# One substitution for both head groups in the delta-net stage of a two-block kernel, and its late weight splits on VectorE

## The chip, the cores and the metric

The kernel runs on one core of one Trainium2 chip. The metric is the device time of one execution in microseconds (us). The engines are named as in the profile: PE is TensorE, DVE is VectorE, ACT is ScalarE, POOL is GpSimd, SP is SyncE, which issues the transfers from memory. PEld is PE's weight load.

## The reference

Two transformer blocks run over 512 tokens of width 1024. The second one adds 16 learned tokens in front, runs a SwiGLU, a mixer and another SwiGLU. The mixer adds a latent attention and a gated delta net, each with a sigmoid gate. The change lies in the delta net, which works on chunks of 64 tokens with 8 heads of 64:

```python
lmat = jnp.where(tri_strict, jnp.einsum('bhncd,bhnsd->bhncs', kb, kc) * decay, 0.0)
eye = jnp.eye(CHUNK, dtype=jnp.float32)
tmat = lax.linalg.triangular_solve(eye + lmat, jnp.broadcast_to(eye, lmat.shape),
                                   left_side=True, lower=True)
u_c = tmat @ (vc * bc[..., None])
w_c = tmat @ (kb * jnp.exp(gc)[..., None])
intra = jnp.einsum('bhncd,bhnsd->bhncs', qc, kc) * decay

def step(state, inp):
    q_i, k_i, u_i, w_i, g_i, a_i = inp
    v_new = u_i - w_i @ state
    o_i = (q_i * jnp.exp(g_i)[..., None]) @ state + a_i @ v_new
    ...
```

Beside it, in the same stretch of the kernel, the gates (`gate_mla`, `gate_gdn`, `z`) are dense products of the normalized hidden state with parts of `w_in`.

## The kernel before, in words

**Precision of the dense products.** A weight tile `raw` of 128x1024 is split in two parts: ACT writes `wh` (rounded), and another engine writes `wl = raw - wh`. Every dense product is three matmuls (`wh` with the high and the low part of the input, `wl` with the high part). `Ctx.stock` (line 434) makes the splits ahead of use: two `raw` tiles may be in flight, and `wh` and `wl` have three buffers each, so a new `wh` waits until PE has finished the weight three places before. The list `mix_items` (line 1493) gives the order of the weights, and its last field says which engine makes `wl`: `None` is DVE, `po` is POOL.

**The delta-net stage.** `gdn` (line 2039) runs 10 units: five token tiles `t` (the first has 16 tokens, the others 128, two chunks each) for each of two head groups `G` of four heads. Unit `u` is `2 t + G`. Each unit passes six generators:

- `prep_a`: POOL makes `gr`; PE transposes k, q (`ptm`) and v (`ptv`); PE sums the decays (`pd`) and ACT makes `E = exp`; DVE and POOL make `vk`, `kb`, `qn`, `qe`, `kd`.
- `prep_b`: PE transposes `kb`, `qn` (`ptb`), ACT copies them to `kqT`, PE multiplies (`pkq`), DVE makes `LT` (the strictly lower matrix, transposed) and `AT`.
- `base`: inverts the 16x16 diagonal blocks of `LT` by substitution. POOL cuts the blocks out (`lm`), DVE folds them into `L16`. Then come 15 steps of three dependent DVE instructions (`STREAM_SHUFFLE XR<-X`, `XR<-XR,L`, `X<-X,XR`), which work on four heads and 1 to 15 columns, so on 4 to 60 elements in each of 128 partitions. POOL spreads the result into `TT`.
- `inverse`: two levels that join blocks: PE transposes `TT` (`ptt`), ACT copies to `Tm`, PE multiplies with `CT` (made by POOL), ACT copies to `Pm`, PE multiplies (`pr`), DVE subtracts from `TT`.
- `factors`: PE makes `pu` (the u and w of the reference), ACT copies to `uw`.
- `scan`: the recurrence over chunks with the state `S` (`pws`, `vn`, `pS`, `po`), then norm and gate of the output.

**The fill.** `filler` (line 1702) is a seventh generator beside them. It issues the dense products `mm<-x,wh` of the z and gate columns (24 matmuls of 512 columns for each weight tile), and then of `w_o2`. DVE multiplies each finished product (`z` or `gate <- mm,bcu`) and ACT applies tanh.

**What sets the order.** Every instruction is emitted by a planner (`Ctx.run`, line 377, and `Clock.pump`, line 185) that holds a clock with costs for each engine. A generator's step runs when the planner finds its inputs ready; the generators are ranked `scan, factors, inverse, base, prep_b, prep_a, fill`. Each engine then runs its own list strictly in that order, and waits on semaphores for the others. The costs know nothing of two engines that slow each other down. Pools give buffers by tag: a tile of a tag waits until the oldest one of that tag has been read for the last time.

Of the kernel before, what the change touches and what calls it, by code (L numbers as in the profile page):

```python
# [10 lines left out]
F32 = mybir.dt.float32  # L11
# [3 lines left out]
ALU = mybir.AluOpType  # L15
AX = mybir.AxisListType  # L16
PSUM = bass.MemoryType.PSUM

P = 128
D = 1024  # L20
KT = D // P
S = 512
NM = 16
T = S + NM
# [1452 lines left out]


HM = 8
DEEP = 3  # L1480

GATES = 3


def b3(ap, n, axis=2):

    sh = list(ap.shape)
    v = ap.unsqueeze(axis)
    sh.insert(axis, n)
    return v.to_broadcast(sh)  # L1490


def mix_items(c):
    po = c.nc.gpsimd
    it = [("w_mix", m, 0, 1024, None) for m in (2, 0, 1, 3)]
    it += [("w_mix", m, 0, 1024, po) for m in [*range(4, 16), *range(20, 20 + GATES), *range(16, 20), *range(20 + GATES, 36)]]
    it += [("w_o2", m, o, 512, None) for o in (0, 512) for m in range(KT)]
    it += [("w_mo", m, 0, 1024, None) for m in range(KT)]
    return it
# [539 lines left out]
def gdn(c, keep, pool, psp, st):  # L2039
# [25 lines left out]
    U = {}  # L2065
# [4 lines left out]
    def prep_a():  # L2070
        yield ("setup",)
        for u, (t, G) in enumerate(units):
            if u >= DEEP:
                yield ("factors", u - DEEP)
            if u > 3:
                yield ("scan", u - 4)
            to, n = TT_B[t]
            ts_, hs = slice(to, to + n), hb(G)
            na = 2 if t else 1

            gr = pool.tile([P, 4, P], F32, tag="gr", name=c.nm("gr"))
            nc.gpsimd.tensor_tensor(
                out=gr[:n, :, :n].rearrange("p (a b) m -> p a b m", a=2),
                in0=b3(b3(M_incl[:n, :n], 2, 1), 2, 1), in1=b3(par_of(g[:n, t, hs]), n, 3), op=ALU.mult)

            kq = pool.tile([P, 2, 4, 64], F32, tag="kq", name=c.nm("kq"))
            yield from room("ga")
            pt = PS("ga", "ptm")
            for i, nm in enumerate("kq"[:na]):
                for f in range(2):  # L2090
                    c.tr(pt[:n, (2 * i + f) * P : (2 * i + f + 1) * P], st[nm][2 * G + f][:, ts_], c.ident)
            nc.scalar.copy(kq[:n, :na].rearrange("p a h d -> p (a h d)"), pt[:n, : 256 * na])
            yield from room("ga")
            pv = PS("ga", "ptv")
            for f in range(2):
                c.tr(pv[:n, f * P : f * P + P], st["v"][2 * G + f][:, ts_], c.ident)
            vk = pool.tile([P, 4, 2, 64], F32, tag="vk", name=c.nm("vk"), bufs=DEEP)
            kd = tok("kd", 4)
            nc.vector.tensor_mul(vk[:n, :, 0], pv[:n, :256].rearrange("p (h d) -> p h d", h=4), b3(beta[:n, t, hs], 64, 2))
            if u:  # L2100
                yield ("E", u - 1)
            yield from room("ga", gr)
            E = pool.tile([P, 4, P], F32, tag="E", name=c.nm("E"))
            pd = v4(PS("ga", "pd"))[:n, :, :n]
            c.mm(pd, M_after[:n, :n], gr[:n, :, :n], True, False)
            c.mm(pd, identb[:n, :n], b3(nmb[:n, :n], 4, 1), False, True)
            nc.scalar.activation(E[:n, :, :n], pd, AF.Exp)
            kb = tok("kb")
            nc.vector.tensor_mul(kb[:n], kq[:n, 0], b3(sc[0][:n, t, hs], 64, 2))
            d = U[u] = dict(vk=vk, kd=kd, E=E, kb=kb)  # L2110
            if t:
                qn, qe = d["qn"], d["qe"] = tok("qn"), tok("qe", DEEP)
                nc.vector.tensor_mul(qn[:n], kq[:n, 1], b3(sc[3][:n, t, hs], 64, 2))
                nc.gpsimd.tensor_tensor(out=vk[:n, :, 1], in0=kq[:n, 0], in1=b3(sc[1][:n, t, hs], 64, 2), op=ALU.mult)
                nc.gpsimd.tensor_tensor(out=qe[:n], in0=kq[:n, 1], in1=b3(sc[4][:n, t, hs], 64, 2), op=ALU.mult)
            nc.gpsimd.tensor_tensor(out=kd[:n], in0=kq[:n, 0], in1=b3(sc[2][:n, t, hs], 64, 2), op=ALU.mult)
            c.mark(("tok", u), kb, *([qn] if t else []))

    def prep_b():
        for u, (t, G) in enumerate(units):  # L2120
# [4 lines left out]
            E = d["E"]  # L2125
            na = 2 if t else 1

            kqT = pool.tile([P, 2, 2, P], F32, tag="kqT", name=c.nm("kqT"))
            yield from room("gb")
            pt = PS("gb", "ptb").rearrange("p (f a m) -> p f a m", f=2, a=2)  # L2130
            for f in range(2):
# [20 lines left out]

    def base():

        for u, (t, G) in enumerate(units):
            yield ("LT", u)
            n, d = TT_B[t][1], U[u]
            r = 32 if t == 0 else P
            X, R_, L16 = (pool.tile([P, 4, 16], F32, tag=x_, name=c.nm(x_)) for x_ in ("X", "XR", "L16"))
            if t:  # L2160
                lm = v4(c.cp.tile([P, T], F32, tag="h7", name=c.nm("lm"))[:, :S])
                nc.gpsimd.tensor_tensor(out=lm, in0=d["LT"], in1=b3(blk[:, 24:], 4, 1), op=ALU.mult)
                nc.vector.tensor_reduce(out=L16, in_=lm.rearrange("p h (b i) -> p h i b", i=16), op=ALU.add, axis=AX.X)
            else:
                nc.gpsimd.memset(L16[:r], 0.0)
                nc.vector.tensor_mul(L16[:n], d["LT"][:n, :, :n], b3(blk[:n, 24 : 24 + n], 4, 1))
            nc.gpsimd.tensor_copy(X[:r], b3(blk[:r, 8:24], 4, 1))
            for i in range(15, 0, -1):
                o = slice(i, 16)
                nc.vector.stream_shuffle(R_[:r, :, o], X[:r, :, o], [16 * (q // 16) + i for q in range(32)])  # L2170
                nc.vector.tensor_mul(R_[:r, :, o], R_[:r, :, o], L16[:r, :, i : i + 1].to_broadcast([r, 4, 16 - i]))
                nc.vector.tensor_sub(X[:r, :, o], X[:r, :, o], R_[:r, :, o])
            TT = pool.tile([P, 4, P], F32, tag="TT", name=c.nm("TT"), bufs=3)
            if t:
                nc.gpsimd.tensor_tensor(out=TT.rearrange("p h (b i) -> p h b i", i=16), in0=b3(X, 8, 2),
                                        in1=b3(b3(blk[:, :8], 16, 2), 4, 1), op=ALU.mult)
            else:
                nc.gpsimd.tensor_copy(TT[:n, :, :n], X[:n])
            d["TT"] = TT
            c.mark(("base", u), TT)  # L2180
            if t == 0:
                c.mark(("inv", u), TT)
            st["based"] = u == len(units) - 1
            yield

    second = lambda a, b: a.rearrange("p q (k two b) -> p q k two b", two=2, b=b)[:, :, :, 1, :]

    def inverse():

        for u, (t, G) in enumerate(units):  # L2190
# [3 lines left out]
            for i in range(2 if t else 0):  # L2194
                CT = pool.tile([P, 4, P], F32, tag="CT", name=c.nm("CT"), bufs=2)
                nc.gpsimd.tensor_tensor(out=CT, in0=LT, in1=b3(lev[:, i, :], 4, 1), op=ALU.mult)
                Tm = pool.tile([P, 4, P], F32, tag="Tm", name=c.nm("Tm"), bufs=2)
                yield from room("gi", TT)
                pt_ = v4(PS("gi", "ptt"))
                for q in range(4):  # L2200
# [3 lines left out]
                pp = v4(PS("gi", "pp"))  # L2204
                for q in range(4):
                    c.mm(pp[:, q], CT[:, q], Tm[:, q], True, True)
                Pm = pool.tile([P, 4, P], F32, tag="Pm", name=c.nm("Pm"), bufs=2)
                nc.scalar.copy(Pm, pp)
                b = 16 << i
                yield from room("gi", Pm)  # L2210
# [379 lines left out]
```

## Time and profile before

| | us |
|---|---|
| median of 3 runs | 2119.61 (2118.64 to 2121.54) |
| the profiled execution | 2118.18 |
| its span, first to last instruction | 2116.4 |
| delta-net stage within the span | 1366 to 1672 |

The page gives each engine's busy time as a share of the span. The stretch that the change touches lies between 1366 us, where the attention of the mixer has ended, and 1672 us, where the products of `w_o2` for the latent attention are done. In a timeline a row begins with start and duration in us; in brackets stands how long the engine sat idle before it, and who released it. In a group by shape the mean duration is in ns. [...]

### The profile page before, as it was taken

The numbers are of one execution on the slowest core, as the hardware profiler recorded it, in microseconds if no ns is written. First come the engines' busy times: TensorE is split into PE (matmuls) and PEld (weight loads), VectorE is DVE, ScalarE is ACT, GpSimd is POOL, SyncE is SP. The second block draws the span as 40 slices with busy tenths as digits, with TensorE's granted clock in tenths as the row PEclk, the third lists the DMA queues.
The fourth block names the chain that finished last, engine by engine and source line by source line (L and its number), as shares of the span: only waits on it lengthen the run. The fifth ranks groups of instructions, "written<-read, shape, count | busy, mean of one in ns | idle before, by whom it ended". The sixth has DMA issues, their size and how long they took to land. (4 is left out here: it accounts for less than half of the span.)

```text
span 2116.4 us, 30687 instructions
## 1 busy us (share of the span) xinstructions
PE 2028.2 (96%) x12029; PEld 1755.6 (83%) x12029; DVE 1198.3 (57%) x2503; ACT 848.1 (40%) x1615; POOL 482.7 (23%) x399
## 2 busy tenths in 40 slices
PE   8999999979999989999999999988889999999998
PEld 6888888867888889999999988856667788888887
DVE  5665564388667573333333677588897653434333
ACT  4444443266565552222222576522233342323222
POOL 3111110154343050000010444344553220000000
PEclk9999999989999999999999999999999999999999
DMA  4222222321211212222224210122001742222332
GB/s 153 80 81 80 80 78 73 100 80 61 70 61 57 90 63 90 91 90 90 85 91 151 74 51 31 56 65 75 16 31 41 248 145 96 93 100 90 93 102 75
DMA packets 61728, 178.67 MB, mean 84 GB/s; under 512 B 8400, under 2 KB 11600, under 8 KB 61584
## 3 DMA queue, kind: packets, MB, share of 16 engines
q1 hardware_dynamic: 60208, 175.54, 25.6%
q8 instruction: 94, 1.54, 0.3%
q10 hardware_dynamic: 1376, 1.18, 0.2%
q14 instruction: 50, 0.41, 0.1%
HBM read 166.21 MB, written 10.49 MB: 83 GB/s over the span
## 5 line engine op out<-in xcount | busy, mean ns | idle before, releaser
L415 PE MATMUL mm<-x,wh 128*128 128x264 f32 (+2 forms) x3536 | 876.6, 344 | 24.6 <-ACT x L254 11.5
L415 PEld LDWEIGHTS mm<-x,wh 128*128 128x128 f32 x3536 | 586.8, 191 | 99.1 <-ACT x L254 12.4
L254 ACT CAST wh<-raw 128x1024 fp32r<-128x1024 f32 (+2 forms) x307 | 306.0, 997 | 698.5 <-PE mm L415 532.6
L415 PE MATMUL mm<-x,wl 128*128 128x264 f32 (+2 forms) x1768 | 552.6, 343 | 2.1 <-DVE wl L254 2.0
L254 DVE TENSOR_TENSOR wl<-raw,wh 128x1024 fp32r<-128x1024 f32 (+3 forms) x248 | 290.7, 1173 | 221.1 <-ACT wh L254 215.7
L415 PEld LDWEIGHTS mm<-x,wl 128*128 128x128 f32 x1768 | 316.8, 191 | 37.5 <-DVE wl L254 2.4
L254 POOL TENSOR_TENSOR acc<-acc,sq 128x512 f32<-128x512 f32 (+4 forms) x73 | 81.4, 1116 | 830.4 <-ACT sq L254 542.9
L415 PE MATMUL mm<-hh,wh 128*128 128x264 f32 (+2 forms) x1100 | 226.6, 315 | 0.0
L415 PEld LDWEIGHTS mm<-hh,wh 128*128 128x128 f32 x1100 | 169.3, 189 | 12.6
L254 POOL TENSOR_TENSOR wl<-raw,wh 128x1024 fp32r<-128x1024 f32 x59 | 141.7, 2404 | 130.3 <-ACT wh L254 124.9
L415 PE MATMUL pvg<-wh,x 128*128 128x512 f32 x512 | 170.7, 397 | 0.0
L415 PE MATMUL mm<-hh,wl 128*128 128x264 f32 (+2 forms) x550 | 143.8, 314 | 0.0
L254 POOL TENSOR_TENSOR ra<-ra,rb 128x512 f32<-128x512 f32 x32 | 57.6, 1800 | 253.1 <-DVE rb L254 253.1
L254 DVE TENSOR_TENSOR t<-mm,t 128x528 f32<-128x528 f32 (+1 forms) x44 | 30.7, 700 | 148.7 <-PE mm L415 148.6
L415 PEld LDWEIGHTS pvg<-wh,x 128*128 128x128 f32 x512 | 96.3, 188 | 20.7
L415 PE MATMUL pvg<-wl,x 128*128 128x512 f32 x256 | 100.4, 392 | 0.0
L254 DVE TENSOR_TENSOR t<-mm,bc 128x528 f32<-128x528 f32 (+1 forms) x42 | 29.4, 700 | 121.5 <-PE mm L415 121.5
L415 PEld LDWEIGHTS mm<-hh,wl 128*128 128x128 f32 x550 | 92.0, 188 | 6.5
L254 ACT ACTIVATE e<-psc,mx 128x128 f32<-128x128 f32 (+7 forms) x104 | 52.1, 508 | 28.1 <-DVE mx L254 22.7
L254 DVE TENSOR_TENSOR XR<-XR,L 128x4 f32<-128x4 f32 (+9 forms) x150 | 57.0, 380 | 3.7
L254 DVE SCALAR_TENSOR_TENSOR x<-h,par,x 128x256 fp32r<-128x256 f32 (+3 forms) x72 | 51.7, 748 | 12.8 <-ACT x L254 12.6
L415 PEld LDWEIGHTS pvg<-wl,x 128*128 128x128 f32 x256 | 48.2, 188 | 9.3
(409 smaller groups left out, 3206.9 us busy)
## 6 DMA issues: line engine op xcount, KB each, us to landing
raw<-in_wg_dram SPq DMA_DIRECT2D x44, 512.0 KB, 3.3
raw<-in_wu_dram SPq DMA_DIRECT2D x44, 512.0 KB, 3.3
raw<-in_w_mix_dram SPq DMA_DIRECT2D x36, 512.0 KB, 3.7
raw<-in_w_ret_vg_dram SPq DMA_DIRECT2D x32, 512.0 KB, 3.7
raw<-in_wd_dram SPq DMA_DIRECT2D x32, 512.0 KB, 3.5
raw<-in_w_dif_kq_dram SPq DMA_DIRECT2D x16, 512.0 KB, 3.7
raw<-in_w_ret_qk_dram SPq DMA_DIRECT2D x14, 512.0 KB, 3.6
raw<-in_w_ret_o_dram SPq DMA_DIRECT2D x13, 512.0 KB, 3.7
```

The source lines that it names most:

```text
L254: p = Op(lambda: f(*a, **k), self.key, cost, tail, i, o, c.before(o), c.rank, c.t)
L415: return self.nc.tensor.matmul(out, lhsT, rhs, start=start, stop=stop, **kw)
```

## The change

It edits only the mixer:

- `base` runs once for each token tile instead of once for each unit: the tiles `X`, `XR` and `L16` hold eight heads, the 15 steps work on 8 to 120 elements, and both units of the tile get their `TT` afterwards. The substitution needs `LT` of both units.
- `DEEP` is 4 instead of 3: four buffers for `vk`, `qe` and `LT`, so `prep_a` may run four units ahead of `factors`.
- The weights 16 to 19 (z) and 23 to 35 (13 of the 16 gates) get `None`: 17 splits `wl` move from POOL to DVE. The weights 4 to 15 and 20 to 22 stay on POOL.
- `E` shares the place of `gr`, `kqT` that of `kq`, and `Pm` that of `Tm` (three buffers for both, before two each). `prep_a` therefore waits for the use of the last unit's `E` before it makes `gr`; it did so before making `E`.

```diff
-DEEP = 3
+DEEP = 4
...
-    it += [("w_mix", m, 0, 1024, po) for m in [*range(4, 16), *range(20, 20 + GATES), *range(16, 20), *range(20 + GATES, 36)]]
+    it += [("w_mix", m, 0, 1024, po) for m in [*range(4, 16), *range(20, 20 + GATES)]]
+    it += [("w_mix", m, 0, 1024, None) for m in [*range(16, 20), *range(20 + GATES, 36)]]
...
+            if u:
+                yield ("E", u - 1)
             gr = pool.tile([P, 4, P], F32, tag="gr", name=c.nm("gr"))
...
-            if u:
-                yield ("E", u - 1)
             yield from room("ga", gr)
-            E = pool.tile([P, 4, P], F32, tag="E", name=c.nm("E"))
+            E = pool.tile([P, 4, P], F32, tag="gr", name=c.nm("E"))
...
-            kqT = pool.tile([P, 2, 2, P], F32, tag="kqT", name=c.nm("kqT"))
+            kqT = pool.tile([P, 2, 2, P], F32, tag="kq", name=c.nm("kqT"))
...
-        for u, (t, G) in enumerate(units):
-            yield ("LT", u)
...
+        for t, (_, n) in enumerate(TT_B):
+            r = P if t else 32
+            X, R_, L16 = (pool.tile([P, 8, 16], F32, tag=x_, name=c.nm(x_)) for x_ in ("X", "XR", "L16"))
+            nc.gpsimd.tensor_copy(X[:r], b3(blk[:r, 8:24], 8, 1))
+            for G in range(2):
+                yield ("LT", 2 * t + G)
...
             for i in range(15, 0, -1):
                 o = slice(i, 16)
                 nc.vector.stream_shuffle(R_[:r, :, o], X[:r, :, o], [16 * (q // 16) + i for q in range(32)])
-                nc.vector.tensor_mul(R_[:r, :, o], R_[:r, :, o], L16[:r, :, i : i + 1].to_broadcast([r, 4, 16 - i]))
+                nc.vector.tensor_mul(R_[:r, :, o], R_[:r, :, o], L16[:r, :, i : i + 1].to_broadcast([r, 8, 16 - i]))
                 nc.vector.tensor_sub(X[:r, :, o], X[:r, :, o], R_[:r, :, o])
...
+            for G in range(2):
+                u, x_ = 2 * t + G, X[:, hb(G)]
+                TT = U[u]["TT"] = pool.tile([P, 4, P], F32, tag="TT", name=c.nm("TT"), bufs=3)
...
-                Tm = pool.tile([P, 4, P], F32, tag="Tm", name=c.nm("Tm"), bufs=2)
+                Tm = pool.tile([P, 4, P], F32, tag="Tm", name=c.nm("Tm"), bufs=3)
...
-                Pm = pool.tile([P, 4, P], F32, tag="Pm", name=c.nm("Pm"), bufs=2)
+                Pm = pool.tile([P, 4, P], F32, tag="Tm", name=c.nm("Pm"), bufs=3)
```

The planner lays all engines' lists anew from this. The number of matmuls stays the same, and so do the matmuls of the fill that stand ahead of the last transpose of the stage (460 before, 461 now). Three places follow.

POOL, where the substitution of units 2 and 3 ends and their joining begins. Before, `wl` of a late weight stands between almost all steps:

```order
L254 TENSOR_TENSOR TT_14385<-X_14381,blk 128x512
L254 COPY X_14575<-blk 128x64
L254 TENSOR_TENSOR wl_14795<-raw_14609,wh_14794 128x1024
L254 TENSOR_TENSOR CT_14819<-LT_14313,lev 128x512
L254 TENSOR_TENSOR wl_14856<-raw_14721,wh_14855 128x1024
L254 TENSOR_TENSOR CT_14894<-LT_14313,lev 128x512
L254 TENSOR_TENSOR TT_14579<-X_14575,blk 128x512
L254 COPY X_14778<-blk 128x64
L254 TENSOR_TENSOR wl_14958<-raw_14796,wh_14957 128x1024
```

Now both units' `TT` come one after the other, and no split is left on POOL:

```order
L254 TENSOR_TENSOR TT_14567<-X_14272,blk 128x512
L254 TENSOR_TENSOR TT_14569<-X_14272,blk 128x512
L254 TENSOR_TENSOR CT_14819<-LT_14336,lev 128x512
L254 COPY X_14570<-blk 128x128
L254 TENSOR_TENSOR lm_14835<-LT_14779,blk 128x512
L254 TENSOR_TENSOR CT_14878<-LT_14336,lev 128x512
L254 TENSOR_TENSOR CT_14939<-LT_14467,lev 128x512
```

What moved: the splits are gone from this list, and the first unit's `TT` stands behind a substitution that serves both.

DVE, in the substitution of unit 3 before, with the product of a gate (`gate<-mm`) in between:

```order
L254 STREAM_SHUFFLE XR_14576<-X_14575 128x4x5
L254 TENSOR_TENSOR XR_14576<-XR_14576,L_2394_14577 128x4x5
L254 TENSOR_TENSOR X_14575<-X_14575,XR_14576 128x4x5
L254 STREAM_SHUFFLE XR_14576<-X_14575 128x4x6
L254 TENSOR_TENSOR gate_14797<-mm_14799,bcu 128x512
L254 TENSOR_TENSOR XR_14576<-XR_14576,L_2394_14577 128x4x6
L254 TENSOR_TENSOR X_14575<-X_14575,XR_14576 128x4x6
```

And now, in the substitution of units 2 and 3:

```order
L254 TENSOR_TENSOR XR_14273<-XR_14273,L_2335_14274 128x8x8
L254 TENSOR_TENSOR gate_14592<-mm_14594,bcu 128x512
L254 TENSOR_TENSOR X_14272<-X_14272,XR_14273 128x8x8
L254 TENSOR_TENSOR wl_14675<-raw_14488,wh_14674 128x1024
L254 STREAM_SHUFFLE XR_14273<-X_14272 128x8x9
L254 SCALAR_TENSOR_TENSOR LT_14636<-pkq_14682,rr,E_14605 128x128
L254 TENSOR_TENSOR XR_14273<-XR_14273,L_2335_14274 128x8x9
```

What moved: the steps are twice as wide and half as many, and a split of 128x1024 stands among them, one step behind the product of the gate.

PE, where the two units of the first token tile leave the substitution (`pu` needs `TT`). Before:

```order
L415 MATMUL mm_14422<-x_9931,wh_14244 128x512
L415 MATMUL pu_14429<-vk_14107,TT_14197 16x64 x4
L419 MATMUL ptm_14438<-ident,cv_11117 128x128
L419 MATMUL ptm_14438<-ident,cv_11118 128x128
L419 MATMUL ptm_14438<-ident,cv_11121 128x128
L419 MATMUL ptm_14438<-ident,cv_11122 128x128
L415 MATMUL mm_14422<-x_9930,wl_14245 128x512
L415 MATMUL mm_14422<-x_10090,wh_14244 128x512
L415 MATMUL mm_14422<-x_10091,wh_14244 128x512
L415 MATMUL pS_14454<-uw_14428,kd_14108 128x128 x2
```

Now:

```order
L415 MATMUL mm_14491<-x_10251,wh_14314 128x512
L415 MATMUL pu_14508<-vk_14110,TT_14269 16x64 x4
L415 MATMUL pu_14514<-vk_14200,TT_14271 16x64 x4
L415 MATMUL pkq_14520<-kqT_14461,cv_11117 128x256
L415 MATMUL pkq_14520<-kqT_14461,cv_11118 128x256
L415 MATMUL pS_14527<-uw_14507,kd_14111 128x128 x2
L415 MATMUL pS_14531<-uw_14513,kd_14201 128x128 x2
L415 MATMUL mm_14491<-x_10252,wh_14314 128x512
```

What moved: the two `pu` stand together, later in the fill (behind 126 fill matmuls counted from the first `ptm`; before, the first stood behind 97 and the second behind 150), and `pS` follows without fill in between.

## Rows read from the trace of the kernel before

**Rows 1.** The page: busy time of each engine; granted clock in 40 slices

```profile
PE 2028.2 (96%) x12029; PEld 1755.6 (83%) x12029; DVE 1198.3 (57%) x2503; ACT 848.1 (40%) x1615; POOL 482.7 (23%) x399
...
PEclk9999999989999999999999999999999999999999
```

**Rows 2.** Busy time by stretch: us, engines with instruction counts, PEclk, DMA share, GB/s

```profile
1366.00:1672.00 306.00, 269.85 (x1404) 209.42 (x1404) 238.17 (x874) 88.50 (x172) 135.01 (x152) 0.93 0.20 64
1366.00:1490.00 124.00, 101.88 (x466) 73.82 (x466) 96.14 (x358) 31.39 (x54) 57.83 (x57) 0.91 0.19 62
1490.00:1672.00 182.00, 167.97 (x940) 135.60 (x940) 142.03 (x516) 57.12 (x119) 77.18 (x95) 0.95 0.20 65
1640.00:1672.00 32.00, 31.13 (x146) 25.01 (x145) 16.94 (x33) 8.62 (x15) 3.20 (x6) 1.00 0.69 227
```

**Rows 3.** Whom PE waited for, 1366 to 1672: us, times, longest

```profile
PE pS L415 <- DVE vn L254: 6.9, 3, 4.7
PE pr L415 <- ACT Pm L254: 4.7, 1, 4.7
...
PE pd L415 <- DVE X L254: 3.8, 1, 3.8
PE pu L415 <- POOL TT L254: 3.6, 2, 1.8
...
PE ptt L419 <- DVE TT L254: 0.4, 2, 0.2
```

**Rows 4.** The timelines of POOL, DVE, ACT and PE around 1454 to 1465

```profile
1453.73 2.39 POOL L254 TENSOR_TENSOR wl<-raw,wh 128x1024 fp32r<-128x1024 f32 x1
...
1458.40 2.38 POOL L254 TENSOR_TENSOR wl<-raw,wh 128x1024 fp32r<-128x1024 f32 x1 [1.03 <-ACT wh L254]
...
1454.02 2.13 DVE L254 TENSOR_TENSOR XR<-XR,L 128x4 f32<-128x4 f32 x1
...
1457.84 0.17 DVE L254 TENSOR_TENSOR X<-X,XR 128x8 f32<-128x8 f32 x1
...
1458.45 2.35 DVE L254 TENSOR_TENSOR X<-X,XR 128x12 f32<-128x12 f32 x1
...
1463.03 0.69 DVE L254 TENSOR_TENSOR gate<-mm,bcu 128x512 f32<-128x512 f32 x1
...
1463.76 0.63 ACT L254 ACTIVATE gate<-gate 128x512 f32<-128x512 f32 x1 [5.43 <-DVE gate L254]
1464.29 0.57 ACT L254 COPY Pm<-pp 128x512 f32<-128x512 f32 x1
...
1464.91 1.97 PE L415 MATMUL pr<-TT,Pm 128*128 128x64 f32 x8 [4.75 <-ACT Pm L254]
```

**Rows 5.** Instructions on XR by stretch; then groups by shape, 1366 to 1672

```profile
1366.00:1672.00 306.00, 138.85 (x600) 0.93 0.20 64
...
L254 DVE STREAM_SHUFFLE XR<-X 128x60 f32<-128x60 f32 x8 | 1.8, 223 | 0.0
...
L254 DVE TENSOR_TENSOR X<-X,XR 128x60 f32<-128x60 f32 x8 | 1.7, 215 | 0.1
```

**Rows 6.** POOL's groups by shape, 1366 to 1672: busy us, mean ns

```profile
L254 POOL TENSOR_TENSOR wl<-raw,wh 128x1024 fp32r<-128x1024 f32 x16 | 38.0, 2375 | 31.7 <-ACT wh L254 31.4
L254 POOL TENSOR_TENSOR CT<-LT,lev 128x512 f32<-128x512 f32 x16 | 20.7, 1294 | 0.4
...
L254 POOL TENSOR_TENSOR gr<-gm,gg 128x512 f32<-128x512 f32 x8 | 8.5, 1062 | 2.1 <-PE pd L415 2.1
...
L254 POOL TENSOR_TENSOR qe<-kq,sc 128x256 f32<-128x256 f32 x8 | 5.1, 638 | 0.0
```

**Rows 7.** DVE's splits by shape, 1672 to 2110; waits, 1366 to 1672

```profile
L254 DVE TENSOR_TENSOR wl<-raw,wh 128x1024 fp32r<-128x1024 f32 x68 | 83.7, 1231 | 76.4 <-ACT wh L254 73.9
...
ACT wh L254 <- PE mm L415: 38.7, 16, 5.2
...
POOL wl L254 <- ACT wh L254: 31.4, 8, 9.9
```

More of the change, by code (lines that the diff above doesn't have):

```diff
@@ L2153, in base @@
     def base():
-        for u, (t, G) in enumerate(units):
-            yield ("LT", u)
[L2157 to L2167, printed above, removed]
+        for t, (_, n) in enumerate(TT_B):
[4 more added lines that the diff above has]
+                yield ("LT", 2 * t + G)
+                LT, l = U[2 * t + G]["LT"], L16[:, hb(G)]
+                if t:
+                    lm = v4(c.cp.tile([P, T], F32, tag="h7", name=c.nm("lm"))[:, :S])
+                    nc.gpsimd.tensor_tensor(out=lm, in0=LT, in1=b3(blk[:, 24:], 4, 1), op=ALU.mult)
+                    nc.vector.tensor_reduce(out=l, in_=lm.rearrange("p h (b i) -> p h i b", i=16), op=ALU.add, axis=AX.X)
+                else:
+                    nc.gpsimd.memset(l[:r], 0.0)
+                    nc.vector.tensor_mul(l[:n], LT[:n, :, :n], b3(blk[:n, 24 : 24 + n], 4, 1))
             for i in range(15, 0, -1):
@@ L2170, in base @@
                 nc.vector.stream_shuffle(R_[:r, :, o], X[:r, :, o], [16 * (q // 16) + i for q in range(32)])
-                nc.vector.tensor_mul(R_[:r, :, o], R_[:r, :, o], L16[:r, :, i : i + 1].to_broadcast([r, 4, 16 - i]))
+                nc.vector.tensor_mul(R_[:r, :, o], R_[:r, :, o], L16[:r, :, i : i + 1].to_broadcast([r, 8, 16 - i]))
                 nc.vector.tensor_sub(X[:r, :, o], X[:r, :, o], R_[:r, :, o])
[L2173 to L2184, printed above, removed]
+            for G in range(2):
+                u, x_ = 2 * t + G, X[:, hb(G)]
+                TT = U[u]["TT"] = pool.tile([P, 4, P], F32, tag="TT", name=c.nm("TT"), bufs=3)
+                if t:
+                    nc.gpsimd.tensor_tensor(out=TT.rearrange("p h (b i) -> p h b i", i=16), in0=b3(x_, 8, 2),
+                                            in1=b3(b3(blk[:, :8], 16, 2), 4, 1), op=ALU.mult)
+                else:
+                    nc.gpsimd.tensor_copy(TT[:n, :, :n], x_[:n])
+                c.mark(("base", u), TT)
+                if t == 0:
+                    c.mark(("inv", u), TT)
+                st["based"] = u == len(units) - 1
+                yield
     second = lambda a, b: a.rearrange("p q (k two b) -> p q k two b", two=2, b=b)[:, :, :, 1, :]
```

## The prediction, made before the changed kernel ran

> **What bounds the kernel now.** I read the page first: PE is busy 96% of the span, so a change pays only where PE idles or runs slowly, and the granted clock falls mainly in the slices of the delta-net stage [rows 1]. The table of stretches puts a size on it [rows 2]. Of the 306 us from 1366 to 1672, PE is busy 269.85 and idle 36.2. [...] By halves: 22.1 us idle and 0.09 x 124 = 11 us of clock from 1366 to 1490, then 14.0 and 0.05 x 182 = 9 us up to 1672. The last 32 us are dense (31.13 busy, clock 1.00): the end of this stage is fill on PE, not the delta net's chain, and behind it the same work follows in both kernels.
>
> Then I asked whom PE waited for [rows 3]: a list of 15 pairs (the first four and the last stand there), nearly all ending in DVE, or in ACT or POOL just behind DVE. The longest single wait shows the mechanism [rows 4]. POOL runs a weight split `wl` from 1453.73 and again from 1458.40, 2.4 us each. While they run, two substitution instructions on DVE take 2.13 and 2.35 us, where a neighbour of nearly the same size takes 0.17. DVE works its list in order, so the product of the gate starts only at 1463.03, ACT's tanh waits for it 5.43 us, the copy to `Pm` stands behind the tanh, and `pr` makes PE idle 4.75 us. Nothing in PE's list can pass it. So the delta net costs PE time through DVE, and DVE is late because POOL holds it up; the planner's costs know nothing of that.
>
> **Part 1, the substitution.** All its DVE instructions together are busy 138.85 us in 600 rows [rows 5], 150 of them mask loads of next to nothing. At 60 elements an instruction takes 0.215 to 0.223 us [rows 5], at 8 elements 0.17 when alone [rows 4]: about 0.95 ns per element. Before, 450 instructions of 32 elements on average: 450 x 0.193 = 87 us. So some 52 us of the 138.85 are hold-ups. After, 225 instructions of 64 elements on average, extrapolated to 120: 225 x 0.223 = 50 us. DVE gains 37 us outright. The price: a unit's `TT` comes only after `LT` of both units and one pass of 45 x 0.223 = 10 us, where it was 8.7 for itself alone. In PE's list that is why the first `pu` stands behind 126 fill matmuls, not 97. The fill covers it, since its total is the same; were the pass later than planned, PE would idle at the `pu` and first `ptt` of each pass. Two such waits of 1.8 us exist now [rows 3]; one of about 2 us for each of the first passes stays inside what I leave below.
>
> **Part 2, the 17 late splits.** On POOL one takes 2.375 us [rows 6], 16 of them in the stretch for 38.0 us. On DVE one of 128x1024 takes 1.231 us [rows 7], so DVE gets 17 x 1.231 = 21 us. What they stop costing: of the 52 us of hold-ups at least their share of POOL's busy time, 38.0 of 135 [rows 2, 6], or 15 us; at most 16 x 2.2 = 35 us, if each holds one instruction for nearly its whole length. I take 25, the middle, since both splits of [rows 4] did hold one. The other 27 us come from what stays on POOL (`CT`, 16 x 1.294 us [rows 6], and its like); with half as many instructions to hold I leave 14. DVE's busy time becomes 238 - 37 - 25 - 13 + 21 = 184 us of the stretch.
>
> The splits bring a new wait. DVE stands at `wl` until ACT has made `wh`, and `wh` waits for PE to give back a buffer: ACT waited 38.7 us for that in 16 cases, and POOL 31.4 us for `wh` in 8 [rows 7]. On POOL little stood behind it; on DVE the next substitution step does, then `LT`, `vn` and `S`, for which PE waits. In DVE's new list the split stands a step behind the gate's product, which needs the same end of a weight on PE. The product (0.69 us [rows 4]) and the step take 0.9 us, the `wh` a little over 1: some 0.3 us of waiting each, 5 us in all, plus the 1.23 us that the chain stands still. Bounds: 0 when PE has fill to do meanwhile, 17 x 1.5 = 26 us when every one reaches PE. I take 4, near the low end, because 24 matmuls of fill lie around each.
>
> **Part 3, buffers and shared places.** Four `DEEP` buffers let preparation run ahead; no gain by itself, since no wait in the list of 15 is for `vk` or `LT`. `gr` now waits for the last use of `E`, and `kqT` for three products on POOL of 0.64 us like `qe` [rows 6], 2 us for a unit. Bounds 0 and 8 x 2 = 16 us; 5 to 20 fill matmuls lie ahead of `pkq` and `pd` in PE's list, so I take 1.
>
> **The sum.** The first half has the longest waits, of the kind in [rows 4], where a split meets the substitution, so I let three quarters of its 33 us go (25). In the second half inverse and scan of several units share DVE with the substitution, and I let only 45% of 23 go (10). The clock goes with the idle time, because in the first half it fell where PE idled most. Less 4 and 1 for the new waits: 30 us. The profiled execution of 2118.2 becomes 2088; the median of the runs stands 1.4 higher, which I leave inside the rounding: 2088.
>
> [...] `CT` on POOL takes 1.294 us on average [rows 6]; the two-operand instructions of VectorE beside it are short, 0.17 to 0.22 us when alone [rows 4, 5]. [...]
>
> **The rivals.** (B) *The hold-up changes sides.* DVE's splits delay POOL's `CT`, `TT`, `lm` and `S`, and are delayed by them, so that PE's waits end on POOL instead. Price: up to 17 x 1.23 = 21 us of the 30. For it: `pu` already waits for POOL's `TT` [rows 3]. Against: without splits POOL is busy only 97 us of the stretch. Time: 2118 - 12 = 2106. (C) *Everything goes*: hold-ups below the slack that the fill gives, idle time under 6 us, clock near 1.00: 2118 - 48 = 2070. (D) *Slower: DVE stands behind ACT behind PE.* DVE inherits POOL's 31.4 us of waiting for `wh` [rows 7], on the chain; only the 25 us of hold-ups by the splits are won back and 3 us of clock are lost: 2118 + 31 - 25 + 3 = 2127. It decides where a split on DVE waits over 1.5 us on average. Against: those waits were long because POOL had nothing else to do. (E) *Nothing arrives*: the steps, now bunched with less fill between, wait for each other as long as they waited for DVE: 2118.
>
> **How the numbers follow.** What can be told from no change here is about 0.2%, 4 us. Chances: forecast (2076 to 2098) 0.55, B 0.22, C 0.10, D 0.07, E 0.06. A seventh of B lies within 0.2%. Faster by over 0.2%: 0.55 + 0.19 + 0.10 = 0.84; within: 0.03 + 0.06 = 0.09; slower: 0.07. The range from 2068 to 2110 takes in the forecast, most of B and of C, and leaves out D, E and the rest.
>
> **What would show it.** In the changed kernel's profile: PE idle below 18 us and clock at 0.96 or more in this stage; all instructions on `XR` together 60 to 80 us busy; 17 splits on DVE at 1.2 to 1.6 us, waiting for `wh` under 10 us together; POOL busy under 100 us. B would show `CT`, `TT` or `S` on POOL well over their times here and PE's waits ending on POOL. D would show DVE idle at `wl` for 20 us or more. I am wrong if PE's waits stay near 36 us although the instructions on `XR` are no longer held.

## The result, and the profile after

The changed kernel takes 2067.4 us (median of 4 runs, 2065.6 to 2068.7) where the kernel before took 2119.1 in the same runs. The ratio is 0.976, with a 95% interval from 0.974 to 0.978: 52 us, or 2.4%, faster. The forecast was 2088; the measured median lies 0.6 us under the low end of its range, and close to the 2070 of rival C, which had one chance in ten.

The profiled execution took 2068.66 us, with a span of 2066.8. From its page, the rows that answer to [rows 1]:

```profile
PE 2006.4 (97%) x12029; PEld 1744.8 (84%) x12029; DVE 1150.0 (56%) x2220; ACT 848.6 (41%) x1615; POOL 445.4 (22%) x377
...
PEclk9999999999999999999999999999999999999999
```

PE has the same 12029 matmuls and 22 us less busy time. The slices of PEclk are too coarse for the stage (before, their one 8 lay in the ninth, from 423 us). Busy time by stretch follows, as in [rows 2] (us, engines PE, PEld, DVE, ACT, POOL with instruction counts, granted clock as a share of full speed, DMA share, GB/s). Since the stage is shorter, it now ends at 1623.5, at the place in the work that stood at 1672 before:

```profile
1366.00:1623.50 257.50, 252.15 (x1434) 199.69 (x1434) 187.11 (x592) 88.85 (x174) 100.90 (x133) 1.00 0.23 77
1366.00:1490.00 124.00, 121.41 (x681) 93.58 (x681) 94.15 (x311) 42.73 (x80) 49.97 (x67) 1.00 0.21 72
1490.00:1623.50 133.50, 130.74 (x756) 106.11 (x755) 92.96 (x281) 46.13 (x95) 50.93 (x67) 1.00 0.25 83
```

PE's idle time falls from 36.2 to 257.5 - 252.15 = 5.35 us, which gives 31 us. For the clock the two stretches can't be compared as they stand: 1434 matmuls lie in this one and 1404 in that of [rows 2], since the changed execution stands a little further back in its work at 1366 us. With the same 1429 matmuls in both, all but one, the stage is this (PE's busy us, before and then after; the rows also count the few that reach over their edges):

```profile
1362.40:1671.80 309.40, 273.25 (x1432) 0.93 0.20 65
```

```profile
1366.20:1623.40 257.20, 251.84 (x1433) 1.00 0.23 77
```

It took 309.4 us and takes 257.2. The same matmuls were busy for 273.25 us at a clock of 0.93 and are busy for 251.84 at 1.00, which gives 21 us beside the 31 of idle time. These 52 us are 3 more than the 49.5 between the two profiled executions: the changed one reaches the stage 3.8 us later and is 1.2 us faster behind it. Why it is late there isn't shown; 2.2 of the 3.8 us have arisen by 1150 us already.

Whom PE still waits for in the stage (us, times, longest), five of seven pairs, against the 15 pairs of [rows 3]:

```profile
PE ptb L419 <- DVE qn L254: 1.5, 3, 1.1
PE ptt L419 <- DVE TT L254: 1.2, 2, 1.1
...
PE pu L415 <- POOL TT L254: 0.6, 1, 0.6
PE pkq L415 <- DVE XR L254: 0.4, 1, 0.4
...
PE ptb L419 <- DVE kb L254: 0.3, 1, 0.3
```

The longest wait is 1.1 us, where it was 4.75. The instructions on `XR` (as [rows 5]), then the groups by shape of DVE's widest step, its splits, and POOL's `CT` (as [rows 5 to 7]; busy us, mean ns):

```profile
1366.00:1623.50 257.50, 61.82 (x300) 1.00 0.23 77
```

```profile
L254 DVE TENSOR_TENSOR wl<-raw,wh 128x1024 fp32r<-128x1024 f32 x16 | 22.3, 1391 | 0.2 <-ACT wh L254 0.2
L254 POOL TENSOR_TENSOR CT<-LT,lev 128x512 f32<-128x512 f32 x16 | 21.5, 1350 | 10.0 <-PE pp L415 9.7
...
L254 DVE TENSOR_TENSOR X<-X,XR 128x120 f32<-128x120 f32 x4 | 1.1, 277 | 0.1
```

Half as many instructions on `XR` are busy for 61.82 us, not 138.85. The widest step takes 0.277 us, as the prediction's 0.95 ns per element gives. The 16 splits in the stretch take 1.391 us each on DVE and wait 0.2 us for `wh`, all of them together. POOL's `CT` takes 1.350 us where it took 1.294, and POOL is busy 100.9 us, where the prediction's sign was under 100.

### The profile page after: what moved, and what is told of

Read it like the earlier page. It is cut to its first block, busy times and chain, and to the rows that moved or that the text cites. A ratio compares the mean times of both kernels' runs of the same rounds, so it can differ in the third digit from the quotient of the medians.

```text
span 2066.8 us, 30398 instructions
## 1 busy us (share of the span) xinstructions
PE 2006.4 (97%) x12029; PEld 1744.8 (84%) x12029; DVE 1150.0 (56%) x2220; ACT 848.6 (41%) x1615; POOL 445.4 (22%) x377
## 5 line engine op out<-in xcount | busy, mean ns | idle before, releaser
L254 DVE TENSOR_TENSOR wl<-raw,wh 128x1024 fp32r<-128x1024 f32 (+2 forms) x265 | 314.7, 1188 | 219.7 <-ACT wh L254 214.1
L254 POOL TENSOR_TENSOR wl<-raw,wh 128x1024 fp32r<-128x1024 f32 x42 | 101.1, 2410 | 91.8 <-ACT wh L254 86.7
L415 PEld LDWEIGHTS pvg<-wh,x 128*128 128x128 f32 x512 | 96.3, 188 | 20.7
L254 ACT ACTIVATE x<-h,par 128x256 fp32r<-128x256 f32 (+3 forms) x72 | 39.8, 577 | 38.9 <-DVE h L254 29.8
```

The lines of the kernel that those rows point to most:

```text
L254: p = Op(lambda: f(*a, **k), self.key, cost, tail, i, o, c.before(o), c.rank, c.t)
L415: return self.nc.tensor.matmul(out, lhsT, rhs, start=start, stop=stop, **kw)
```

## The experiments

The change has three parts. Part 1 is the joint substitution, part 2 the late splits on VectorE, and part 3 the four buffers with the shared places. The first runs put them together in all ways; the later ones take a single cause by itself. All times are medians, all ratios against the kernel before on the same chip, with the 95% interval.

| | parts | us | ratio |
|---|---|---|---|
| before | none | 2114.8 to 2119.1 | 1 |
| d_only | 3 | 2120.9 | 1.0014 (1.0005 to 1.0024) |
| s_only | 1 | 2115.5 | 0.9999 (0.9986 to 1.0011) |
| w_only | 2 | 2089.3 | 0.9876 (0.9853 to 0.9898) |
| after_sep | 2, 3 | 2087.7 | 0.9856 (0.9833 to 0.9879) |
| ws | 1, 2 | 2108.9 | 0.9960 (0.9945 to 0.9975) |
| after_d3 | 1, 2, shared places, three buffers | 2111.8 | 0.9968 (0.9955 to 0.9982) |
| after_pool | 1, 3 | 2096.3 | 0.9902 (0.9883 to 0.9920) |
| changed kernel | 1, 2, 3 | 2067.4 | 0.9761 (0.9742 to 0.9781) |

### One part, and two, at a time

**Part 2 alone (w_only)**, the kernel before with the line of the splits:

```diff
-    it += [("w_mix", m, 0, 1024, po) for m in [*range(4, 16), *range(20, 20 + GATES), *range(16, 20), *range(20 + GATES, 36)]]
+    it += [("w_mix", m, 0, 1024, po) for m in [*range(4, 16), *range(20, 20 + GATES)]]
+    it += [("w_mix", m, 0, 1024, None) for m in [*range(16, 20), *range(20 + GATES, 36)]]
```

> The kernel before with Part 2 alone: the 17 late weights' wl on VectorE, substitution still unit by unit, three buffers, no shared places. Theory A (POOL's 2.4 us splits hold VectorE, and what is held beyond the fill's slack makes PE idle and its clock fall): the largest hold goes, 26 of some 59 us of held time on VectorE in 1366 to 1672; PE idle in the stage falls from 36 to about 15, the clock to about 0.97: 2080 to 2092. Theory R1 (VectorE's own load on the chain is what counts: 450 narrow steps, and now 17 x 1.23 = 21 us more): 2112 to 2130, PE still waiting for instructions behind XR and X. Theory R2 (the new order and deeper buffers do it, both parts only together): 2105 to 2118.

It took 2089.3 us, as theory A expected. The stretch 1366 to 1672 of its trace:

```profile
1366.00:1672.00 306.00, 284.58 (x1527) 220.24 (x1526) 250.93 (x916) 102.82 (x192) 116.18 (x141) 0.99 0.28 92
```

Idle time falls from 36.2 to 21.4 us and the clock rises from 0.93 to 0.99. This stretch ends 32 us behind the stage, so DVE's 250.93 us hold work of the next one. With the same matmuls as before (1361.8 to 1640.2 us here) DVE executes 892 instructions, not 876, and is busy for 227.8 us, not 238.4: the splits came in, and the instructions on `XR` fell from 138.85 to 112.73 us. R1, by which the 450 narrow steps and the splits added to them decide, expected 2112 us or more, and is out.

**Part 1 alone (s_only)**, the kernel before with the function `base` of the changed kernel:

```diff
-        for u, (t, G) in enumerate(units):
-            yield ("LT", u)
...
+        for t, (_, n) in enumerate(TT_B):
...
+            for G in range(2):
+                yield ("LT", 2 * t + G)
```

> The kernel before with Part 1 alone: one substitution for both head groups, the late splits still on POOL at 2.4 us, three buffers, no shared places. Theory A: half as many narrow instructions can still be held by 16 splits of 2.4 us; those held stand on one chain for two units now. Instructions on XR fall from 139 to 75 to 90 us, PE idle from 36 to 20 to 28, clock 0.94 to 0.96: 2095 to 2110. Theory R1 (VectorE's load): 37 us less of it, and nothing added: 2078 to 2092. Theory R2: 2105 to 2118.

It took 2115.5 us, no change. Theory A missed, and so did R1: the 37 us less of work on DVE arrive (the instructions on `XR` are busy 69.39 us, not 138.85), but not at the end. The time lies in R2's range, but R2 missed part 2 alone by 16 us and misses after_pool, below, by more; what is right in it is that the buffers matter. PE's stretch 1366 to 1590 and the one behind it:

```profile
1366.00:1590.00 224.00, 210.31 (x1124) 0.97 0.22 73
1590.00:1672.00 82.00, 61.30 (x313) 0.79 0.19 61
```

Up to 1590 the clock is 0.97 and PE idles 13.7 us. Then PE idles 20.7 of 82 us and the clock is 0.79. What is won early is lost in the last quarter of the stage.

**Parts 1 and 2 (ws)**, the two diffs together, without part 3.

> Parts 1 and 2 together, without Part 3: three buffers for vk, qe and LT, and E, kqT and Pm in places of their own. Theories A and R1: within 3 us of the changed kernel, 2065 to 2071, since no wait in the lists was for a buffer of vk or LT. Theory R2 (buffers and the order that they allow carry the gain): 2080 to 2100, with PE waiting in the stage for work that starts later.

It took 2108.9 us. Each theory missed: A and R1 by 38 us, R2 by 9. Part 1 put onto part 2 costs 20 us (2089.3 to 2108.9) unless part 3 stands beside it, and with part 3 it gains 20 (after_sep to the changed kernel, below).

**Parts 1 and 3 (after_pool)**, the changed kernel with the old line of the splits:

```diff
-    it += [("w_mix", m, 0, 1024, po) for m in [*range(4, 16), *range(20, 20 + GATES)]]
-    it += [("w_mix", m, 0, 1024, None) for m in [*range(16, 20), *range(20 + GATES, 36)]]
+    it += [("w_mix", m, 0, 1024, po) for m in [*range(4, 16), *range(20, 20 + GATES), *range(16, 20), *range(20 + GATES, 36)]]
```

> The changed kernel with the 17 late splits back on POOL. Theory A: as Part 1 alone, 2090 to 2110, with VectorE's instructions on XR and X held up to 2.3 us again and low clock in the stage. Theory R1: 2060 to 2068, faster than the changed kernel, since VectorE has 21 us less to do. Theory R2: within 3 us of the changed kernel, 2065 to 2071.

It took 2096.3 us, as theory A expected. Without part 2 the changed kernel loses 29 us, about what part 2 gains on the kernel before (28).

### What the four buffers do

**Three buffers (after_d3)**, the changed kernel with one number changed:

```diff
-DEEP = 4
+DEEP = 3
```

> The changed kernel with DEEP 3: vk, qe and LT have three buffers, and the preparation of a unit waits for pu of the unit three back; shared places stay. The run with Parts 1 and 2 alone took 2108.9, and in it the substitution of one token tile began only after pu of the tile before (at 1424, 1478, 1536 and 1594 us), so that PE ran out of fill and waited for the chain from 1597 on. Theory D (the depth of four takes this link out of the chain): passes begin every 55 us again, low clock at the end of the stage, 2100 to 2112. Theory P (the shared places and the gr that waits for the last E reorder the preparation): within 4 us of the changed kernel, 2063 to 2071.

It took 2111.8 us, as theory D expected. Beside parts 1 and 2 the shared places bring nothing; it is the fourth buffer that lets part 1 pay. First PE in three stretches of this run, then the fill and other products (`mm`) alone:

```profile
1366.00:1590.00 224.00, 219.10 (x1181) 0.99 0.26 88
1590.00:1672.00 82.00, 55.27 (x276) 0.69 0.09 27
1600.00:1665.00 65.00, 38.71 (x191) 0.64 0.09 29
```

```profile
1597.00:1672.00 75.00, 7.44 (x23) 0.66 0.09 30
```

And PE's longest waits from 1590 to 1672:

```profile
PE ptt L419 <- POOL TT L254: 6.7, 1, 6.7
PE pto L419 <- DVE to L254: 4.4, 2, 3.6
PE pto L419 <- DVE XR L254: 4.1, 1, 4.1
```

From 1597 to 1672 only 7.44 us of `mm` are left: in PE's list all 527 matmuls of the fill stand ahead of `pu` of unit 7. Only the chain's own small matmuls remain, each waiting for the next, and PE is busy 38.71 of 65 us at a clock of 0.64. The changed kernel has 72 of its 461 fill matmuls left behind `pu` of unit 7, its last transpose of the stage starts at 1603 us, and from 1597 to 1672 PE is busy with `mm` for 71.56 us, at 1.00:

```profile
1597.00:1672.00 75.00, 71.56 (x302) 1.00 0.71 239
```

Why the chain is late is seen where the last pass begins. `prep_a` of unit u is let go only when `factors` of unit u - DEEP is planned. A joint pass needs `LT` of units 2t and 2t + 1, so with three buffers the pass of tile t waits for `factors` of unit 2t - 2, and thus for the pass of the tile before. With four it is unit 2t - 3, from one pass earlier. POOL in the run with three buffers, from the pass of units 6 and 7 (`TT`) to the last pass, where the `gr` is that of unit 9:

```profile
1571.74 2.52 POOL L254 TENSOR_TENSOR TT<-X,blk 128x512 f32<-128x512 f32 x2 [11.02 <-DVE X L254]
...
1578.18 1.48 POOL L254 TENSOR_TENSOR gr<-gm,gg 128x512 f32<-128x512 f32 x1
...
1601.48 1.31 POOL L254 TENSOR_TENSOR lm<-LT,blk 128x512 f32<-128x512 f32 x1 [1.14 <-DVE LT L254]
```

And in the changed kernel, where `gr` of unit 9 stands ahead of `TT` of units 6 and 7, and `lm` of unit 9 follows `TT` by 4.5 us, not by 30:

```profile
1524.21 1.04 POOL L254 TENSOR_TENSOR gr<-gm,gg 128x512 f32<-128x512 f32 x1
...
1534.51 2.07 POOL L254 TENSOR_TENSOR TT<-X,blk 128x512 f32<-128x512 f32 x2 [7.54 <-DVE X L254]
...
1539.02 1.30 POOL L254 TENSOR_TENSOR lm<-LT,blk 128x512 f32<-128x512 f32 x1
```

With three buffers the last four passes begin at 1434, 1488, 1545 and 1602 us, some 56 us apart; in the changed kernel at 1421, 1449, 1508 and 1539.

**One unit at a time (after_sep)**, the changed kernel with the old `base`, and **part 3 alone (d_only)**, which has the old line of the splits (the diff of after_pool) as well:

```diff
-        for t, (_, n) in enumerate(TT_B):
+        for u, (t, G) in enumerate(units):
+            yield ("LT", u)
```

> The changed kernel with the substitution unit by unit as before (Parts 2 and 3 without Part 1). Theory D: depth pays only where a pass waits for two units; one unit at a time needs no fourth buffer, so this is Part 2 alone, 2083 to 2093, and the joint pass brings the 20 us from there to the changed kernel by 37 us less of VectorE's work on the chain. Rival (depth lets the chain start earlier whatever the substitution): 2064 to 2075, and the joint pass brings next to nothing.

> Part 3 alone: four buffers and the shared places in the kernel before, with the substitution unit by unit and the late splits on POOL. Theory D (depth pays only with a joint pass): no change, 2113 to 2121. Rival (depth is a gain of its own, some 20 us, and Part 1 adds next to nothing to it): 2094 to 2104.

They took 2087.7 and 2120.9 us, both as theory D expected: the fourth buffer is worth nothing by itself, and nothing beside part 2. It pays only together with the joint pass.

### Is it the hold?

A hold means here that an instruction of DVE or POOL lasts longer because of what the other one runs beside it. Part 2 takes the splits' hold from DVE, but it also moves work between lists and lets the planner lay all lists anew. In the next two kernels every engine's list is that of the kernel before, word for word, except that a late split on POOL is executed as a narrow subtraction and a MEMSET (one in **b_fill1**, two in **b_fill2**):

```diff
+                f(*a, **{n: x[:, :cut] if is_ap(x) else x for n, x in k.items()})
+                self.eng.memset(k["out"][:, cut:].bitcast(F32), 0.0)
+                self.eng.memset(k["out"][:, cut:].bitcast(F32), 0.0)
```

> The kernel before with every engine's order kept word for word; only the execution of the 17 late splits is changed: POOL subtracts 32 of 1024 columns, after the same wait for wh, and a MEMSET writes zero to the other 992, which leaves most of the low part of those weights out. A MEMSET of 256 columns took 0.31 us and one of 8 columns 0.10 on POOL, so I estimate 0.9 us for it and 1.1 us for both, where the split took 2.4. Theory H (POOL's reading of two operands holds VectorE; a MEMSET reads none): the 26 us of VectorE held under splits go, 2085 to 2100. Rival Q (not VectorE is late but POOL: CT, TT and lm stand in its list behind 2.4 us): half of that, 2095 to 2108. Rival O (the gain of Part 2 alone came from the new order of the lists): 2112 to 2120, since the order is the old one.

> As the run before, but with the MEMSET twice, so that POOL is busy for some 2.1 us in place of each late split while it reads almost nothing. Theory H: within 4 us of the run with one MEMSET, and instructions on XR and X short beside the MEMSETs. Rival Q: 2108 to 2118, since POOL's list is as late as before. A third reading, that a MEMSET holds VectorE like a split: instructions on X and XR of 0.9 us or more beside MEMSETs, and no gain over before in this run, some in that with one. Rival O: 2112 to 2120 in both.

They took 2089.5 us (0.987, 0.984 to 0.989) and 2083.9 us (0.983, 0.982 to 0.985). POOL's groups in the second, in the stage:

```profile
L259 POOL MEMSET wl<- 128x992 f32 x16 | 15.1, 946 | 0.9
L258 POOL MEMSET wl<- 128x992 f32 x16 | 14.8, 926 | 0.0
...
L257 POOL TENSOR_TENSOR wl<-raw,wh 128x32 fp32r<-128x32 f32 x16 | 4.1, 257 | 21.0 <-ACT wh L256 20.8
```

The three instructions sum to 2.13 us for one split, against 2.375, so POOL is nearly as busy as before, and yet the time is that of part 2 alone or better (5.6 us better than with one MEMSET, where theory H expected at most 4). Rival Q (POOL's late list), rival O (the new order) and the third reading (a MEMSET holds like a split) are out. That zeros stand in most of the low part isn't the reason either, as far as a run shows it: the same zeros leave the changed kernel's time as it is (a_fill, below). DVE and POOL side by side show why. Timelines of POOL and DVE in b_fill2 (start, duration):

```profile
1455.71 0.93 POOL L258 MEMSET wl<- 128x992 f32 x1
1456.69 0.93 POOL L259 MEMSET wl<- 128x992 f32 x1
1457.58 1.32 POOL L256 TENSOR_TENSOR CT<-LT,lev 128x512 f32<-128x512 f32 x1
```

```profile
1456.34 0.17 DVE L256 TENSOR_TENSOR XR<-XR,L 128x8 f32<-128x8 f32 x1
1456.55 0.17 DVE L256 TENSOR_TENSOR X<-X,XR 128x8 f32<-128x8 f32 x1
...
1456.96 0.17 DVE L256 TENSOR_TENSOR XR<-XR,L 128x12 f32<-128x12 f32 x1
...
1457.79 1.15 DVE L256 TENSOR_TENSOR X<-X,XR 128x16 f32<-128x16 f32 x1
```

Beside the MEMSETs (1455.71 to 1457.62) the two-operand steps of the substitution take 0.17 to 0.18 us. The next one, at 1457.79, takes 1.15: behind the MEMSETs POOL has begun a `CT`, which reads two operands. In [rows 4] steps of the same kind took 2.13 and 2.35 us beside a split. Over the whole stage, 13 two-operand steps began while POOL ran a split in the kernel before, and they took 1.95 to 2.36 us each, 28.7 together; the three STREAM_SHUFFLE, with one operand, that did so took 0.17 to 0.19. In b_fill2 19 two-operand steps began beside the three pairs of MEMSETs at 1440.33, 1445.00 and 1455.71 us, and they took 0.17 to 0.19; beside a `CT`, behind the first of these pairs, one took 1.25.

The stage of b_fill2 as a whole, and its instructions on `XR`:

```profile
1366.00:1672.00 306.00, 290.73 (x1565) 225.97 (x1564) 236.43 (x905) 105.38 (x197) 144.78 (x194) 1.00 0.29 96
```

```profile
1366.00:1672.00 306.00, 111.76 (x600) 1.00 0.29 96
```

`XR` falls from 138.85 to 111.76 us: the splits held it for 27. Some 25 us of hold are left there (111.76 less the 87 that the prediction works out for the bare steps), and still PE idles only 15.3 us, not 36.2, at full clock. So about half of the hold went, and with it most of the loss: from 36.2 us of idle time and 21 of clock to 15.3 us at a clock of 1.00. Of the hold that is left, the fill covers at least 10 us.

### What a split costs on VectorE

**Half a test (a_fill)**: the changed kernel with its lists kept, the late splits on DVE executed as a narrow subtraction and a MEMSET:

```diff
-            p = Op(lambda: f(*a, **k), self.key, cost, tail, i, o, c.before(o), c.rank, c.t)
+                f(*a, **{n: x[:, :cut] if is_ap(x) else x for n, x in k.items()})
+                self.eng.memset(k["out"][:, cut:].bitcast(F32), 0.0)
```

> The changed kernel, every engine's order kept; VectorE subtracts 32 of 1024 columns of each late weight and a MEMSET writes zero to the other 992, which leaves most of the low part of those weights out. This prices the 17 splits on VectorE, for which the prediction took 4 us off the gain. If they cost that: 2061 to 2065. If the fill covers them, as PE's 5.4 us of idle time in the stage say: within 0.1% of the changed kernel, 2065 to 2069. If a split on VectorE holds POOL (rival B), CT on POOL falls from 1350 to about 1290 ns and TT from 1125 to 1070.

It took 2068.4 us (0.977, 0.975 to 0.978), the time of the changed kernel. Its groups in the stage, DVE's MEMSET and subtraction and POOL's `CT`:

```profile
L256 POOL TENSOR_TENSOR CT<-LT,lev 128x512 f32<-128x512 f32 x16 | 20.4, 1281 | 9.7 <-PE pp L420 9.4
...
L258 DVE MEMSET wl<- 128x992 f32 x16 | 14.2, 885 | 2.5 <-issue 2.3 <-DVE wl L257 0.2
...
L257 DVE TENSOR_TENSOR wl<-raw,wh 128x32 fp32r<-128x32 f32 x16 | 5.7, 357 | 0.2
```

The two sum to 1.24 us where the split took 1.39, so DVE's load hardly fell and the run can't price it. What it does show is the other side of the hold: `CT` falls from 1.350 to 1.281 us. The splits on DVE held POOL there, for 16 x 0.07 = 1.1 us in all; `TT` on POOL stayed at 1.125. Two instructions of POOL in the changed kernel make up nearly all of the hold, a copy to `X` and a single `CT`:

```profile
1414.26 1.82 POOL L254 COPY X<-blk 128x128 f32<-128x128 f32 x1
...
1536.53 2.28 POOL L254 TENSOR_TENSOR CT<-LT,lev 128x512 f32<-128x512 f32 x1
```

In the same trace the three other copies of this size take 0.28 to 0.29 us and the other 15 `CT` 1.288 on average, which puts the two at 2.5 us of hold; POOL's whole list in the stage is 2.6 us shorter in a_fill (98.29 us busy, not 100.90). The `CT` began while DVE ran a split from 1535.72 to 1537.66 and ended 1.15 us behind it. The copy began 0.01 us ahead of its split by the records and was held all the same. POOL holds the splits in turn: eleven of the 16 take 1.20 to 1.23 us, and the other five, which began while POOL ran a `kd`, a `CT` or a `TT`, 1.41 to 2.23.

**The load doubled (a_twice)**: the same with every late split on DVE executed twice.

```diff
+                f(*a, **k)
+                f(*a, **k)
```

> The changed kernel, every engine's order kept, with each of the 17 late splits executed twice on VectorE, one behind the other: 16 x 1.39 = 22 us more of VectorE in the stage, on the list in which the substitution stands. In the run with a MEMSET in place of the split VectorE had only 2.4 us less to do, so that run could not price this load. Theory S (fill covers delays up to a slack, as in the runs where holds of 39 us were left and PE waited for 8): 2066 to 2072, PE waiting 5 to 10 us in the stage, clock 0.98 or more. Rival (each microsecond more on VectorE reaches PE as the prediction's 4 of 21 did, or more, since the slack is used up): 2072 to 2095, with gaps on PE at pu, ptt or ptb and low clock beside them.

It took 2087.8 us (0.986, 0.983 to 0.989): 20 us more for 16 x 1.293 = 20.7 us on DVE. Theory S fell, and the time lies in its rival's range. The second split, PE's stage (which ends at about 1641 here), and PE's two largest waits:

```profile
L258 DVE TENSOR_TENSOR wl<-raw,wh 128x1024 fp32r<-128x1024 f32 x16 | 20.7, 1293 | 0.6
```

```profile
1366.00:1640.00 274.00, 257.27 (x1415) 0.98 0.21 71
```

```profile
PE ptb L425 <- DVE kb L256: 4.2, 3, 2.4
PE ptt L425 <- DVE TT L256: 3.9, 2, 2.3
```

In 1366 to 1640 PE idles 16.7 us where the changed kernel idles 5.4 (268.64 busy of 274), and the clock falls to 0.98. So the changed kernel has little slack left: the 22 us of splits that its lists were laid for cost at most PE's 5.4 us of idle time, and 21 us that they were not laid for cost 20. On POOL the 32 products on `S` take 14.2 us, not 13.4, so POOL can have a small part in it.

### The other splits of the mixer

**All on VectorE (all_dve)**: the changed kernel, weights 4 to 15 and 20 to 22 moved as well:

```diff
-    it += [("w_mix", m, 0, 1024, po) for m in [*range(4, 16), *range(20, 20 + GATES)]]
-    it += [("w_mix", m, 0, 1024, None) for m in [*range(16, 20), *range(20 + GATES, 36)]]
+    it += [("w_mix", m, 0, 1024, None) for m in [*range(4, 16), *range(20, 20 + GATES), *range(16, 20), *range(20 + GATES, 36)]]
```

> The changed kernel with the other 15 weights of the mixer (4 to 15 and 20 to 22) split by VectorE too; their splits lie from 1150 to 1366 us, where PE idles 5.8 us and the clock is 0.98, so 10 us are lost at most. If what POOL's 35.8 us of splits hold reaches PE there as it did in the delta net: 2058 to 2064. If PE's waits there end in work that no split holds, or VectorE's 153 us in that stretch leave no place for 18 us more: 2065 to 2075.

It took 2073.3 us (0.979, 0.978 to 0.981), 6 us more than the changed kernel, whose interval it touches: no gain, and more likely a small loss. The stretch ahead of the delta net, where these splits lie, and PE's two longest waits in it:

```profile
1150.00:1366.00 216.00, 210.56 (x1698) 192.93 (x1696) 151.19 (x369) 135.91 (x312) 48.24 (x39) 0.97 0.21 68
```

```profile
PE psc L415 <- ACT e L254: 2.6, 1, 2.6
PE mm L415 <- DVE cin L254: 1.9, 1, 1.9
```

PE's idle time there is 5.4 us, as in the changed kernel (5.8), and the wait for `cin` stays, so moving these splits brings nothing there. A wait of 2.6 us for ACT is new. The loss lies behind this stretch: the 1429 matmuls up to the end of the delta net's stage take 263.8 us, not 257.2, with 8.0 us of idle time and a clock of 0.99, while the same number of matmuls ahead of them takes 215 us in both. What in the new lists brings it isn't shown.

## Why the prediction was off, and where it was right

**What bounds the kernel: right, but for one reading.** 22.1 and 14.0 us of idle time and 11 and 9 us of clock were put down for the two halves. The change took 31 us of the idle time and 21 for the clock. That a clock of 0.91 costs 0.09 of the time was the author's estimate; the same 1429 matmuls, busy for 273.25 us at 0.93 and for 251.84 at 1.00, bear it out. That the page's slices show the clock falling in this stage was misread: in [rows 1] their only 8 lies near 450 us, and the table of stretches [rows 2] alone shows the loss.

**The mechanism of part 2: right, and shown.** With the order kept, taking POOL's reads out of the splits alone brings 29 to 34 us (b_fill1, b_fill2); it removes 26 to 27 us of hold on `XR`, where the prediction took 25 between bounds of 15 and 35.

**Part 1's durations: right.** 61.82 us on `XR`, inside the 60 to 80 forecast. DVE's busy time in the stage is 187.11, forecast 184.

**The new wait: sized too high.** The prediction took 5 us of waiting at `wl` for `wh`, and 4 us of price with the standing time of the chain. The row has 0.2 us of waiting, and PE's whole remaining idle time, 5.35 us, is the upper bound of the price. The order of the lists that the planner laid around those splits hides them; it would not hide as many again (a_twice).

**Part 3: the step that failed.** "Four buffers let preparation run ahead; no gain by itself" was right word for word (2120.9 us) and wrong as a term of the sum. It was read from the waits of the kernel before, in which no unit waits for another one's `LT`. Part 1 brings that link in: a joint pass needs the second unit's `LT`, whose preparation is let go by `factors` of the unit three back, which is an output of the pass before. Without the fourth buffer parts 1 and 2 together bring 8 us and not 52. It was luck that the change had the third part in it: the prediction counts on part 1 without it, and part 1 pays only with it.

**The sum: mis-sized.** Three quarters of the first half's loss and 45% of the second's were let go; measured is the loss of each half nearly whole: the first idles 2.6 of 124 us, the second 2.8 of 133.5, both at 1.00. The reason given for the small share was that inverse, scan and substitution share DVE in the second half and would wait on. They do share it, but their delays fall below what the fill hides. Rival C named that, and its 2070 is 2.6 us off; the forecast's 2088 is 20.6 us off.

**The rivals.** B (the hold changes sides) exists as a mechanism, with 2.6 us on POOL in all, 1.1 of them on `CT` (a_fill), where B gave it 12 us of the kernel's time, and of PE's waits only 0.6 us end on POOL. D (DVE waits for `wh`) has 0.2 us against the 31.4 that it took over from POOL. E is out.

**What stays open.** b_fill1 and b_fill2 differ by 5.6 us although PE idles about as long in their stages (13.9 and 15.3 us); the first has a clock of 0.95 there (the row below; busy us as in the other stretches) and the second of 1.00. The loss lies from 1490 to 1672 us, at 0.92, where PE is busy 174.21 of 182 us; b_fill2 has 1.00 there with 171.94. Why the clock is lower in the one with less idle time there is not settled. Nor was it tried what two splits on DVE for each weight would cost if the planner knew of them.

```profile
1366.00:1672.00 306.00, 292.13 (x1514) 228.30 (x1512) 232.97 (x899) 100.70 (x191) 127.33 (x173) 0.95 0.27 90
```

## What to carry to other kernels

Where a planner lays the lists, look for time that its costs don't contain: an instruction that takes 2.13 us next to a twin of 0.17 may be held by another engine, and time on that list reached PE almost one to one here once the planned cover was used up (20 of 20.7 us in a_twice). To prove a hold, keep every list as it is and put an instruction that reads nothing and lasts as long in the place of the one that holds, as the two MEMSETs of b_fill2 did here (2.13 us for 2.375).

Before joining two units of work in one step, follow what lets the second unit start: here the joint step needed one more place in the rings of its inputs (`vk`, `qe` and `LT` grew together; which of them was needed isn't shown), and without it the work saved came back as waiting at the end, where the fill was gone. An edit without effect by itself may be what the others stand on, so price edits in pairs, not from the waits of the kernel before.

## What the runs showed of the hardware

- A MEMSET of 992 columns on POOL (0.93 us) left the narrow two-operand instructions of DVE at 0.17 to 0.19 us beside it (19 in b_fill2), where a `CT` on POOL made two of them 1.15 and 1.25 us long (b_fill2) and a split 1.95 to 2.36 (13 in the kernel before).
- The hold is lopsided here: 16 splits of 2.375 us on POOL held the instructions on `XR` for 27 us, 16 splits of 1.391 us on DVE held POOL for 2.6 us, 1.1 of them on `CT`. POOL has 133 instructions in the changed kernel's stage and DVE 592: two of POOL's made up nearly all of the hold, where 13 narrow steps of DVE began beside a split before.
- In the stage of the kernel before, cut in 306 windows of 1 us, the granted clock was 1.00 in 255 of them and 0.50 in 33. It was 0.64 in a stretch where PE worked on small matmuls between waits and was busy 38.71 of 65 us (after_d3), and 1.00 where the fill stood between such matmuls, with PE busy 121.41 of 124 us (the changed kernel). Idle time alone doesn't tell it: from 1490 to 1672 us, 0.92 with 174.21 of 182 us busy in b_fill1, 1.00 with 171.94 in b_fill2.
